# Zero fills of a dilated attention branch moved from GpSimd to VectorE, and its attention steps issued at more places of the dense work

## The chip, the cores and the metric

The kernel runs on one core of one Trainium2 chip. The metric is device time in microseconds (us) of one execution; several runs are taken and their median is used. One further execution was recorded by the hardware profiler, and all rows below are from that one.

## The reference

One layer of a decoder trunk in float32, 512 tokens of width 1024. Cut to what matters here:

```python
h = _rms(x, norm1_g[layer])
(a_q, a_k, a_v, i_q, i_k, i_w, b_q, b_kv, b_g, c_qkv, mix_g) = _split_last(h @ w_in[layer], IN_SIZES)
y_a = _dsa_attention(...) @ w_branch_a[layer]      # top-128 keys by an index score, 8 heads
y_b = _nsa_attention(...) @ w_branch_b[layer]      # compressed + selected + window, 8 heads
y_c = _dilated_attention(...) @ w_branch_c[layer]  # 3 groups (windows 128, 512, 2048; steps 1, 4, 16) x 4 heads
g = jax.nn.sigmoid(mix_g).reshape(bsz, seq, 3, D_MODEL)
x = x + (g[:, :, 0] * y_a + g[:, :, 1] * y_b + g[:, :, 2] * y_c) @ w_out[layer]
h = _rms(x, norm2_g[layer])
gate, up = jnp.split(h @ w_ffn_in[layer], 2, axis=-1)
x = x + (jax.nn.silu(gate) * up) @ w_ffn_out[layer]
```

## The kernel before

**Dense work.** Every dense product is made of three matmuls on a high and a low part of each operand (`mm3`, lines 103 to 108). Weights come by DMA on SyncE's queue (`weights`, line 84): a tile `raw` of two 128-row chunks is cast to `whi` on ScalarE (line 81) and the rest `wlo` is taken on VectorE or, in some projections, on GpSimd (line 82); `whi` and `wlo` have six buffers each. These have a higher priority than all else.

**Order of the dense work.** After the first norm come the narrow projections, the index queries, the inputs of the compression, the keys and queries of branch B, then the queries of branch A in two projections of four 128-token tiles, and then nine "dilated" projections of four tiles each (`spill`, line 736, which calls `proj_tm`, line 252): six `cqk_tm` and three `cv_tm`. Each tile is copied from PSUM on ScalarE (line 745), and the result goes to HBM. Then come the gates and merges of the branches, in the order B (`bi` 1), A (`bi` 0), C (`bi` 2), eight column blocks each. `gate(bi, f)` computes a gate block and its tanh `tz` (line 956; three buffers of tag `tm`), `merge(bi, f, tz)` multiplies it by the branch's output block (lines 970 to 973). A merge stands one gate later than its own gate. After them are the output projection, the second norm and the feed-forward part.

**Steps of the attention.** Beside the dense work stands a list of generators; `tick()` (line 119) advances each of them by one step. One is `attention()`, which walks through units of one 128-query tile and two heads: first branch B (with the compressed scores between), then branch A, then the preparation (`c_prep`) and the units (`c_unit`) of the dilated branch C. A unit is cut in parts that go to successive steps: scores, table and softmax; transposes and their copies `pT`; and at the end of four units the products with the values (`ovb`, `ova`, line 541; `ovc`, lines 888 and 893). Another generator does the index scores and the top-k of branch A (`select`, line 413: 48 passes, one per step). `tick()` stands once after each projection tile, twice in each gate, and in the merges of A and every second merge of B and C. So the attention's steps 1 to 4 stand in the second query projection of A, 5 to 28 in the `cqk_tm` and 29 to 40 in the `cv_tm` projections, 41 to 44 in B's first two gates. B's last value product is of step 44, A's of step 61; `ready` (line 1008) would issue what is missing before a merge.

**What sets the order on an engine.** The Tile framework orders the instructions of each engine when it compiles: it takes what its own timeline expects to be ready, the earlier in the program's text first (high priority ahead of that), and gives out buffers as it expects them free. A step's place in the text is thus a rank and no barrier, neither forward nor back. On the chip each engine then runs its list in order.

**Zero fills.** `c_prep` makes, for each of two halves and two heads, a tile `pt12` of 128 x (2 x 4 x 128) elements (three buffers) and zeroes it on GpSimd (line 825). The units copy transposed probabilities of groups 1 and 2 into it (lines 876 and 878): query tile `i` writes 32(i + 1) rows of its 128 columns, so the last tile writes all 128 rows. Its memory is that of the pool `ab`, which branches A and B use before.

Of the kernel before, what the change touches and what calls it, by code (L numbers as in the profile page):

```python
# [22 lines left out]
NT = S // 128  # L23
# [8 lines left out]
C_CQ, C_CK, C_CV, C_MIX = 2268, 3036, 3804, 4572  # L32
# [35 lines left out]
def block_kernel(ctx: ExitStack, tc: tile.TileContext, x, norm1_g, norm2_g, w_in, qk_norm_g, cmp_pos, cmp_w,  # L68
                 w_ba, w_bb, w_bc, w_out, w_fi, w_fo, rel_bias, onehot, masks, out):
    nc = tc.nc  # L70
# [13 lines left out]
    def weights(w, segs, kcs, per=2, pool=()):  # L84

        res = {}
        width = sum(n for _, n in segs)
        with tc.high_priority():
            for k0 in kcs[::per]:
                raw = wp.tile([128, per, width], F32, name="raw", tag="raw", bufs=5)  # L90
                o = 0
                for c0, n in segs:
                    nc.sync.dma_start(raw[:, :, o:o + n],
                                      w[k0 * 128:(k0 + per) * 128, c0:c0 + n].rearrange("(k p) c -> p k c", p=128))
                    o += n
                hi = wp.tile([128, per, width], F32R, name="whi", tag="whi")
                lo = wp.tile([128, per, width], F32R, name="wlo", tag="wlo")
                split(hi, lo, raw, nc.gpsimd if pool and k0 // per % 4 in pool else None)
                for j in range(per):
                    res[k0 + j] = (hi[:, j, :], lo[:, j, :])  # L100
        return res

    def mm3(ps, pairs, k0=0, n=None):
        n = n or len(pairs)
        for j, ((ah, al), (bh, bl)) in enumerate(pairs, k0):
            nc.tensor.matmul(ps, ah, bh, start=(j == 0), stop=False)  # L106
            nc.tensor.matmul(ps, ah, bl, start=False, stop=False)  # L107
            nc.tensor.matmul(ps, al, bh, start=False, stop=(j == n - 1))  # L108
# [7 lines left out]
    def start(gen):  # L116
        tasks.append(gen)

    def tick():
        for g in list(tasks):  # L120
            try:
                next(g)
            except StopIteration:
                tasks.remove(g)
# [79 lines left out]
    def mm_tile():  # L204
        return mmp.tile([128, S], F32, name="pm", tag="mm")
# [43 lines left out]
        return bass.AP(tensor=tab.tensor, offset=tab.offset + hi - 1, ap=[list(tab.ap[0]), [-1, hi - lo]])  # L249


    def proj_tm(segs, evac, then=None):
        width = sum(n for _, n in segs)
        wk = weights(w_in, segs, list(range(KC)), pool=PP)
        for t in range(NT):
            ps = mm_tile()
            ts = slice(t * 128, (t + 1) * 128)
            mm3(ps[:, 0:width], [((xh[:, k, ts], xl[:, k, ts]), wk[k]) for k in range(KC)])
            evac(t, ps)
            tick()  # L260
        if then is not None:
            start(then())

# [20 lines left out]
    def tmt(name):  # L284
        return ap_.tile([128, NT, 256], F32, name=name, tag="tm", bufs=3)

    def norm_heads(tm, c0, nh):

        ss = ty.tile([128, 16], F32, name="ss", tag="ss")
        v4 = tm[:, :, c0:c0 + 64 * nh].rearrange("p t (h d) -> p t h d", d=64)  # L290
        for t in range(0, NT, 2):
            sq = ap_.tile([128, 2, 256], F32, name="sq", tag="sq", bufs=1)
            nc.scalar.activation(sq[:, :, 0:64 * nh], tm[:, t:t + 2, c0:c0 + 64 * nh], AF.Square)
            nc.vector.tensor_reduce(out=ss[:, t * nh:(t + 2) * nh].rearrange("p (t h) -> p t h", h=nh),
                                    in_=sq[:, :, 0:64 * nh].rearrange("p t (h d) -> p t h d", d=64), op=ALU.add,
                                    axis=AX.X)
        r = rstd(ss, NT * nh, 1.0 / 64)
        r4 = r[:, 0:NT * nh].rearrange("p (t h) -> p t h", h=nh).unsqueeze(3).to_broadcast([128, NT, nh, 64])
        nc.vector.tensor_tensor(out=v4, in0=v4, in1=r4, op=ALU.mult)
# [432 lines left out]
    dC = dp.tile([6, 128, NT, 256], F32, name="dC")  # L732
    dV = dp.tile([3, S, 256], F32, name="dV")
    cmap = {}

    def spill(name, segs, dst, nh):
        t_ = tmt(name)

        def then():
            if nh:  # L740
                norm_heads(t_, 0, nh)
            nc.sync.dma_start(dst, t_)
            yield

        proj_tm(segs, lambda t, ps: nc.scalar.copy(t_[:, t, :], ps[:, 0:256]), then=then)

    c_in = {}
    c_jobs = [(hf, g, s) for hf in range(2) for g in range(3) for s in "qk"]
# [37 lines left out]
    def c_prep(hf, cz, ld):  # L786
        for g in range(3):
            for s in "qk":
                if hf == 1:
                    c_load()  # L790
                    yield
                t_ = c_in.pop((hf, g, s))
                ps = tr_cols(t_, 0)
                if g == 0:
                    ld[s, g] = (near_queries if s == "q" else near_keys)(hf, cz, ps)
                    if len(c_jobs) > 6:
                        c_load()
                    yield
                    continue
                cq = cz.tile([128, S], F32, name="cq", tag="cq", bufs=8)  # L800
                dst = cq
                if s == "q":
                    dst, ps = cq.rearrange("p (i r w) -> p i r w", i=NT, r=4), ps.rearrange("p (i w r) -> p i r w", i=NT, r=4)
                elif g:
                    dst, ps = cq.rearrange("p (r u) -> p r u", r=4), ps.rearrange("p (u r) -> p r u", r=4)
                nc.scalar.activation(dst, ps, AF.Copy, scale=(gain8[:, 4:5] if s == "q" else gain[:, 5:6]))
                ld[s, g] = cq
                if len(c_jobs) > 6:
                    c_load()
                yield  # L810
            rows = dV[g, :, 128 * hf:128 * hf + 128]
            v_ = cz.tile([128, NT, 128], F32, name="c_v", tag="cv", bufs=6)
            nc.sync.dma_start(v_, rows.rearrange("(u r) c -> u r c", r=NT) if g else
                              rows.rearrange("(t p) c -> p t c", p=128))
            ld["v", g] = v_
        for j in range(2):
            h = 2 * hf + j
            tab = cz.tile([128, S], F32, name="ctab", tag="ctab", bufs=4)
            for r in range(4):
                rows = tab[32 * r:32 * r + 32]  # L820
                vec_table(rows[:, 0:256], 16 + h, V_C0 + r, [[4, 32], [1, 256]])
                vec_table(rows[:, 256:384], 20 + h, V_C1, [[1, 32], [1, 128]])
                vec_table(rows[:, 384:512], 24 + h, V_C2, [[1, 32], [1, 128]])
            pt = cz.tile([128, 2, NT, 128], F32, name="pt12", tag="pt12", bufs=3)
            nc.gpsimd.memset(pt, 0.0)
            ld["tab", j], ld["pt", j] = tab, pt

    def c_unit(hf, i, j, ld, d):
# [130 lines left out]
    def merge(bi, f, tz):  # L959
        nk = KC // 2 if bi < 2 else 2  # L960
        os_ = outs[bi]
        cs = slice(128 * (f % 2), 128 * (f % 2) + 128)
        th, zi = tz[:, 0, :], tz[:, 1, :]
        if f % 2 == 0:
            wys["w"] = weights(wbs[bi], [(f // 2 * 256, 256)], list(range(nk)))
        if bi != 1:
            nc.sync.dma_start(zi, dz[f])
        wy = wys["w"]
        py = mm_tile()
        mm3(py, [((wy[k][0][:, cs], wy[k][1][:, cs]), (os_[k][:, 0, :], os_[k][:, 1, :])) for k in range(nk)])  # L970
        if bi == 0 or f % 2:
            tick()
        nc.vector.scalar_tensor_tensor(out=th, in0=th, scalar=1.0, in1=py, op0=ALU.add, op1=ALU.mult)
        if bi != 1:
            eng = nc.vector if bi == 2 and f > KC - 3 else nc.gpsimd
            eng.tensor_tensor(out=th, in0=th, in1=zi, op=ALU.add)
        if bi != 2:
            nc.sync.dma_start(dz[f], th)
        else:
            nc.scalar.mul(zs["h"][:, f, :], th, 0.5)  # L980
            nc.vector.scalar_tensor_tensor(out=zs["l"][:, f, :], in0=th, scalar=0.5, in1=zs["h"][:, f, :].bitcast(F32),
                                           op0=ALU.mult, op1=ALU.subtract)
# [15 lines left out]
    cn = 0  # L998
    for hf in range(2):
        for g in range(3):  # L1000
            spill("cqk_tm", [(C_CQ + 256 * g + 128 * hf, 128), (C_CK + 256 * g + 128 * hf, 128)], dC[cn], 4)
            cmap["q", hf, g], cmap["k", hf, g] = (cn, 0), (cn, 128)
            cn += 1
    for g in range(3):
        spill("cv_tm", [(C_CV + 256 * g, 256)], dV[g].rearrange("(t p) c -> p t c", p=128), 0)
    zx = ExitStack()

    def ready(bi):
# [19 lines left out]
    for m_ in due:  # L1028
        merge(*m_)
# [78 lines left out]
    for c in range(0, DFF, 256):  # L1108
# [7 lines left out]
        for j in range(2):  # L1116
# [7 lines left out]
            f = c // 128 + j  # L1124
# [40 lines left out]
```

## Time and profile before

| | |
|---|---|
| median of 3 runs | 996.48 us (994.18 to 1000.4) |
| the profiled execution: its time | 995.54 us |
| the profiled execution: first to last instruction | 993.8 us |
| mean granted TensorE clock | 0.993 of full speed |
| TensorE busy | 974.3 us, 98% |
| VectorE, ScalarE, GpSimd busy | 568.1, 437.5, 175.4 us |

1.74 us of the profiled execution lie outside the span. In the rows, PE is TensorE, PEld its weight load, DVE VectorE, ACT ScalarE, POOL GpSimd, SPq the DMA queue of SyncE; L12 is line 12 of the kernel. In a table by stretch each engine has its busy time and, in brackets, its instructions; PEclk is the clock granted, 1.00 for 2.4 GHz and 0.50 for 1.2 GHz.

### The profile page before, as it was taken

To read this page: it belongs to the slowest core of one execution; us is meant where nothing else is said; L and a number is where in the kernel's file an instruction comes from. 1 tells how busy PE (TensorE), PEld (TensorE's weight loads), DVE (VectorE), ACT (ScalarE), POOL (GpSimd) and SP (SyncE) were. 2 spreads that over 40 slices of the span, in tenths; PEclk is the share of its full clock that TensorE was granted. 3 is DMA by queue.
4 is the path that set the end of the run, shared out by engine and by line. 5 is a ranking of instruction groups with operands and counts; after the bars stand their busy time and mean duration, and the time that the engine had idled before them with its cause. 6 is when DMAs were issued, how large, how long until landed. Compare 5 with 4: busy or idle time off the path is not lost.

```text
span 993.8 us, 16076 instructions
## 1 busy us (share of the span) xinstructions
PE 974.3 (98%) x5887; PEld 827.0 (83%) x5887; DVE 568.1 (57%) x1277; ACT 437.5 (44%) x956; POOL 175.4 (18%) x156
## 2 busy tenths in 40 slices
PE   6999999999999999989999999999999999999998
PEld 6889999899887578858777899988888888888886
DVE  6699999766665655665764654544344444422321
ACT  5544555755665555554543434433233233322220
POOL 4135555543100202231110312000000000000000
PEclk9999999999999899989999999999999999999999
DMA  8541344433232334346613462233333323332421
GB/s 210 122 128 44 85 119 132 123 109 122 90 104 67 85 117 138 107 141 193 180 62 97 140 210 86 85 94 108 96 85 105 107 85 91 110 97 96 138 75 42
DMA packets 119264, 109.91 MB, mean 111 GB/s; under 512 B 19931, under 2 KB 105234, under 8 KB 119186
## 3 DMA queue, kind: packets, MB, share of 16 engines
q1 hardware_dynamic: 116994, 107.85, 37.4%
q10 hardware_dynamic: 2192, 1.05, 0.4%
q8 instruction: 46, 0.75, 0.3%
q14 instruction: 32, 0.26, 0.1%
HBM read 96.66 MB, written 12.21 MB: 110 GB/s over the span
## 4 chain that ended last, share of the span: by engine, by line
PE 96%; DMA 1%; DVE 1%; ACT 1%; issue 0%; SPq 0%; DVEq 0%; ACTq 0%
PE pf L108 14%; PE pf L107 14%; PE pf L106 14%; PE pm L107 13%; PE pm L106 13%; PE pm L108 13%; PE tr L111 5%; PE ovb L541 2%; PE lg L363 2%; PE lg L364 2%; PE ova L541 1%; PE lg L843 1%; DMA raw<-in_w_in 1%; PE ovc L888 1%; PE lg L838 0%
## 5 line engine op out<-in xcount | busy, mean ns | idle before, releaser
L82 DVE TENSOR_TENSOR wlo<-raw,whi 128x512 fp32r<-128x512 f32 (+1 forms) x243 | 182.5, 756 | 147.7 <-ACT whi L81 146.6
L81 ACT CAST whi<-raw 128x512 fp32r<-128x512 f32 (+1 forms) x288 | 176.8, 619 | 173.9 <-PE pf L108 78.6
L107 PE MATMUL pm<-wlo,xh 128*128 128x256 f32 (+1 forms) x512 | 145.9, 288 | 0.3 <-DVE wlo L82 0.3
L108 PE MATMUL pm<-whi,xl 128*128 128x256 f32 (+1 forms) x512 | 145.3, 286 | 0.5 <-POOL xl L82 0.5
L106 PE MATMUL pm<-whi,xh 128*128 128x256 f32 (+1 forms) x512 | 145.7, 289 | 0.0
L107 PE MATMUL pf<-xl,whi 128*128 128x512 f32 (+1 forms) x384 | 142.6, 372 | 0.1
L106 PE MATMUL pf<-xh,whi 128*128 128x512 f32 (+1 forms) x384 | 142.5, 372 | 0.0
L108 PE MATMUL pf<-xh,wlo 128*128 128x512 f32 (+1 forms) x384 | 142.0, 371 | 0.0
L107 PEld LDWEIGHTS pm<-wlo,xh 128*128 128x128 f32 x512 | 98.5, 193 | 1.9 <-issue 0.8
L108 PEld LDWEIGHTS pm<-whi,xl 128*128 128x128 f32 x512 | 98.7, 193 | 1.4 <-POOL xl L82 0.8
L106 PEld LDWEIGHTS pm<-whi,xh 128*128 128x128 f32 x512 | 98.3, 194 | 0.4
L107 PE MATMUL pm<-xl,whi 128*128 128x512 f32 x224 | 88.8, 396 | 0.0
L108 PE MATMUL pm<-xh,wlo 128*128 128x512 f32 x224 | 88.6, 395 | 0.0
L106 PE MATMUL pm<-xh,whi 128*128 128x512 f32 x224 | 88.4, 395 | 0.0
L107 PEld LDWEIGHTS pf<-xl,whi 128*128 128x128 f32 x384 | 72.3, 188 | 12.8 <-DVE xl L82 0.3
L108 PEld LDWEIGHTS pf<-xh,wlo 128*128 128x128 f32 x384 | 72.2, 188 | 12.6
L106 PEld LDWEIGHTS pf<-xh,whi 128*128 128x128 f32 x384 | 72.2, 188 | 12.3
L82 POOL TENSOR_TENSOR wlo<-raw,whi 128x512 fp32r<-128x512 f32 x45 | 62.2, 1402 | 111.6 <-ACT whi L81 100.8
L106 PE MATMUL pf<-whi,hh 128*128 128x512 f32 x176 | 69.4, 395 | 0.0
L108 PE MATMUL pf<-whi,hl 128*128 128x512 f32 x176 | 69.4, 395 | 0.0
L107 PE MATMUL pf<-wlo,hh 128*128 128x512 f32 x176 | 69.4, 395 | 0.0
L562 ACT ACTIVATE p<-p,m 128x128 f32<-128x128 f32 (+3 forms) x96 | 53.9, 562 | 28.6 <-DVE m L547 26.4
(312 smaller groups left out, 1702.3 us busy)
## 6 DMA issues: line engine op xcount, KB each, us to landing
raw<-in_w_in SPq DMA_DIRECT2D x92, 256.0 KB, 3.0
raw<-in_w_ffn_in SPq DMA_DIRECT2D x88, 256.0 KB, 2.9
raw<-in_w_ffn_out SPq DMA_DIRECT2D x44, 256.0 KB, 2.8
raw<-in_w_in SPq DMA_DIRECT2D x52, 128.0 KB, 2.4
x<-in_x SPq DMA_DIRECT2D x8, 512.0 KB, 5.9
tab<-dvec SPq DMA_DIRECT2D x16, 256.0 KB, 3.3
dz<-tz SPq DMA_DIRECT2D x16, 256.0 KB, 2.4
tz<-dz SPq DMA_DIRECT2D x16, 256.0 KB, 3.3
```

Of the source, the lines that this page charges most:

```text
L81: nc.scalar.copy(dst_hi, src)
L82: (eng or nc.vector).tensor_tensor(out=dst_lo, in0=src, in1=dst_hi.bitcast(F32), op=ALU.subtract)
L106: nc.tensor.matmul(ps, ah, bh, start=(j == 0), stop=False)
L107: nc.tensor.matmul(ps, ah, bl, start=False, stop=False)
L108: nc.tensor.matmul(ps, al, bh, start=False, stop=(j == n - 1))
L111: nc.tensor.transpose(dst, src, ident[0:src.shape[0], 0:src.shape[0]])
L363: nc.tensor.matmul(lg, qs, k[:, 0, 0:w], start=True, stop=False)
L364: nc.tensor.matmul(lg, qs, k[:, 1, 0:w], start=False, stop=stop)
L541: mm = nc.tensor.matmul(ov[64 * j:64 * j + 64, 128 * b:S], v(b), pts[j][:, 4 * b:3 * b + NT, :], start=first and b == 0, stop=last and b = ...
L562: nc.scalar.activation(p[:, 0:w], p[:, 0:w], AF.Exp, bias=m[:, 0:1], scale=-1.0, accum_out=m[:, 1:2])
L843: nc.tensor.matmul(lg[32 * r:32 * r + 32, c:c + n], ld["q", g][hp, 128 * i + 32 * r:128 * i + 32 * r + 32], ld["k", g][hp, 128 * r:128 * r ...
L888: nc.tensor.matmul(ov[h, 128 * b_:128 * q1], ld["v", 0][:, b_, h], d["pt", jj][:, 2 * b_:b_ + q1, :], start=b_ == 0, stop=False)
```

## The change

1. The zero fill goes to VectorE and covers the first three of the four query tiles (128 x 768 elements for 128 x 1024), since the last tile's columns are written whole.
2. Each of the nine dilated projections has five steps for four: two after its first tile (`more=1`).
3. Every merge has a step: four more in B's merges (the even blocks), and four in C's, where all steps are done by then.

```diff
-    def proj_tm(segs, evac, then=None):
+    def proj_tm(segs, evac, then=None, more=0):
...
-            tick()
+            for _ in range(1 + (t < more)):
+                tick()
...
-    def spill(name, segs, dst, nh):
+    def spill(name, segs, dst, nh, more=0):
...
-        proj_tm(segs, lambda t, ps: nc.scalar.copy(t_[:, t, :], ps[:, 0:256]), then=then)
+        proj_tm(segs, lambda t, ps: nc.scalar.copy(t_[:, t, :], ps[:, 0:256]), then=then, more=more)
...
-            nc.gpsimd.memset(pt, 0.0)
+            nc.vector.memset(pt[:, :, 0:NT - 1, :], 0.0)
...
-        if bi == 0 or f % 2:
-            tick()
+        tick()
...
-            spill("cqk_tm", [...], dC[cn], 4)
+            spill("cqk_tm", [...], dC[cn], 4, 1)
...
-        spill("cv_tm", [(C_CV + 256 * g, 256)], dV[g].rearrange("(t p) c -> p t c", p=128), 0)
+        spill("cv_tm", [(C_CV + 256 * g, 256)], dV[g].rearrange("(t p) c -> p t c", p=128), 0, 1)
```

After it the attention's steps 5 to 34 stand in the `cqk_tm`, 35 to 49 in the `cv_tm` projections, and B's first gate begins with step 50.

## Rows read from the trace of the kernel before

**Rows 1.** The page: the engines' shares, and the chain that ended last, by engine.
```profile
PE 974.3 (98%) x5887; PEld 827.0 (83%) x5887; DVE 568.1 (57%) x1277; ACT 437.5 (44%) x956; POOL 175.4 (18%) x156
PE 96%; DMA 1%; DVE 1%; ACT 1%; issue 0%; SPq 0%; DVEq 0%; ACTq 0%
```

**Rows 2.** The table by stretch over the span up to 990 us: length, busy time of PE, PEld, DVE, ACT and POOL, PEclk, DMA share, GB/s.
```profile
0.00:15.00 15.00, 6.16 (x25) 5.25 (x26) 8.77 (x24) 8.56 (x18) 6.67 (x16) 1.00 0.87 243
15.00:322.00 307.00, 307.00 (x2292) 280.36 (x2292) 237.21 (x603) 172.41 (x421) 107.59 (x79) 1.00 0.39 105
322.00:340.00 18.00, 15.73 (x83) 9.07 (x82) 9.43 (x35) 10.42 (x29) 0.67 (x1) 0.81 0.23 68
340.00:430.00 90.00, 90.00 (x463) 71.68 (x462) 56.66 (x150) 51.17 (x124) 21.52 (x21) 1.00 0.41 120
430.00:446.00 16.00, 11.45 (x54) 6.89 (x53) 10.39 (x19) 7.44 (x17) 4.50 (x6) 0.79 0.53 150
446.00:990.00 544.00, 543.89 (x2979) 453.76 (x2979) 244.94 (x451) 187.54 (x352) 34.45 (x35) 1.00 0.36 109
```

**Rows 3.** The same table inside the two holes.
```profile
326.00:331.20 5.20, 3.57 (x23) 2.49 (x22) 3.57 (x10) 4.20 (x11) 0.59 (x1) 1.00 0.34 104
331.20:338.00 6.80, 6.26 (x24) 3.37 (x26) 1.66 (x6) 1.90 (x5) 0.08 (x1) 0.50 0.13 38
431.90:433.60 1.70, 0.14 (x1) 0.00 (x0) 1.70 (x1) 0.36 (x3) 1.70 (x3) 1.00 0.45 124
433.60:440.20 6.60, 3.93 (x17) 3.13 (x18) 4.60 (x11) 3.25 (x8) 1.58 (x2) 0.50 0.25 75
```

**Rows 4.** The timeline of the second hole (start, duration, engine, line, tile, shapes, and in brackets the idle time of the engine before it and what ended that).
```profile
431.34 1.16 POOL L557 TENSOR_TENSOR tabm<-tab,topm 128x512 f32<-128x512 f32 x1 [0.70 <-DVE m L563]
431.37 4.02 DVE L564 TENSOR_SCALAR p<-p,m 128x384 f32<-128x384 f32 x1
432.44 2.74 POOL L825 MEMSET pt<- 128x1024 f32 x3
435.31 0.67 DVE L547 CUSTOM_DVE_ANT_0 p<-lg,tabm 128x512 f32<-128x512 f32 x1
435.54 0.87 PE L111 MATMUL tr<-ident,p 128*128 128x128 f32 x3 [3.49 <-DVE p L564]
436.59 0.41 DVE L564 TENSOR_SCALAR p<-p,m 128x384 f32<-128x384 f32 x1
```

**Rows 5.** The timeline of VectorE and GpSimd 2 us earlier, where the same operation stands beside one GpSimd operation.
```profile
428.99 1.64 POOL L557 TENSOR_TENSOR tabm<-tab,topm 128x512 f32<-128x512 f32 x1 [0.24 <-DVE m L563]
429.53 1.26 DVE L564 TENSOR_SCALAR p<-p,m 128x256 f32<-128x256 f32 x1
```

**Rows 6.** Groups by line and shape: prices of a fill and of VectorE operations of one result.
```profile
L825 POOL MEMSET pt<- 128x1024 f32 x4 | 3.7, 962 | 10.8 <-PE ovc L893 10.8
L140 DVE MEMSET mhalf<- 128x16 f32 x1 | 0.1, 72 | 0.8 <-PEq L1156 0.8
L547 DVE CUSTOM_DVE_ANT_0 p<-lg,tab 128x128 f32<-128x128 f32 x24 | 6.8, 288 | 16.9 <-PE lg L364 15.0 <-PE tr L111 1.2 <-DMA tab<-dvec 0.7
L547 DVE CUSTOM_DVE_ANT_0 p<-lg,tab 128x512 f32<-128x512 f32 x16 | 10.7, 688 | 9.4 <-PE lg L364 7.0 <-PE tr L111 2.1
```

**Rows 7.** Timelines of single engines, in order of time: the last pass of the top-k; the copies of the 22nd `cqk_tm` tile and of the third and fourth `cv_tm` tile; the first value product of B's third pair; the activation of B's second gate; B's last value product; the activation of B's fourth gate.
```profile
163.33 0.68 DVE L418 MATCH_REPLACE8 work<-m,work 128x512 f32<-128x512 f32 x1
216.29 0.37 ACT L745 COPY cqk_tm<-pm 128x256 f32<-128x256 f32 x1 [0.20 <-PE pm L108]
236.72 0.37 ACT L745 COPY cv_tm<-pm 128x256 f32<-128x256 f32 x1 [0.84 <-PE pm L108]
242.18 0.37 ACT L745 COPY cv_tm<-pm 128x256 f32<-128x256 f32 x1
285.09 2.38 PE L541 MATMUL ovb<-pT,bv 128*64 128x512 f32 x16
298.92 0.60 ACT L956 ACTIVATE tz<-pm 128x512 f32<-128x512 f32 x1
333.18 4.53 PE L541 MATMUL ovb<-pT,bv 128*64 128x512 f32 x16 [0.35 <-ACT pT L530]
344.99 0.60 ACT L956 ACTIVATE tz<-pm 128x512 f32<-128x512 f32 x1 [0.25 <-DMA dz<-tz]
```

**Rows 8.** TensorE's timeline in the middle of the sum of one gate (`pm`), with transposes and scores of B between.
```profile
292.12 0.40 PE L108 MATMUL pm<-xh,wlo 128*128 128x512 f32 x1
292.36 0.71 PE L111 MATMUL tr<-ident,p 128*128 128x128 f32 x5
293.08 0.45 PE L106 MATMUL pm<-xh,whi 128*128 128x512 f32 x1
```

**Rows 9.** The timelines of GpSimd and VectorE at the fourth fill.
```profile
511.18 0.96 POOL L825 MEMSET pt<- 128x1024 f32 x1 [10.76 <-PE ovc L893]
512.48 1.08 DVE L82 TENSOR_TENSOR oT<-ovc,oT 128x512 fp32r<-128x512 f32 x1 [1.23 <-ACT oT L81]
```

**Rows 10.** TensorE's timeline in a gate with nothing between: four dense matmuls follow from 312.76 to 313.44 us, of which the first and the last.
```profile
312.76 0.39 PE L106 MATMUL pm<-xh,whi 128*128 128x512 f32 x1
...
313.44 0.39 PE L106 MATMUL pm<-xh,whi 128*128 128x512 f32 x1
```

More of the change, by code (lines that the diff above doesn't have):

```diff
@@ L1000, in block_kernel @@
         for g in range(3):
-            spill("cqk_tm", [(C_CQ + 256 * g + 128 * hf, 128), (C_CK + 256 * g + 128 * hf, 128)], dC[cn], 4)
+            spill("cqk_tm", [(C_CQ + 256 * g + 128 * hf, 128), (C_CK + 256 * g + 128 * hf, 128)], dC[cn], 4, 1)
             cmap["q", hf, g], cmap["k", hf, g] = (cn, 0), (cn, 128)
```

## The prediction

> **What bounds the kernel now.** I read the shares first: TensorE is busy for 974.3 of 993.8 us, and 96% of the chain that ended last is TensorE [rows 1]. No other engine can set the time, so the question is only where TensorE stands still or runs slowly. The table by stretch answers it: before 15 us it lacks 8.84 us while the first loads come, in the 544 us from 446 on 0.11 us, and nothing in two stretches of 307 and 90 us. What is left, besides the last 4 us of the span, are two holes, 322 to 340 us (2.27 us idle) and 430 to 446 us (4.55 us idle) [rows 2]. Inside each the granted clock falls from 2.4 to 1.2 GHz after TensorE has been partly idle: in the first it was busy for 3.57 of 5.2 us before the fall, in the second for 0.14 of 1.7 us. While low it worked for 6.26 and 3.93 us [rows 3]; at full clock this is half the time, so the low clock cost about 3.1 and 2.0 us. The holes thus cost 2.27 + 3.1 = 5.4 us and 4.55 + 2.0 = 6.5 us, 11.9 us together. That is all that a change of order can give: 995.54 - 11.9 = 983.6 us, 1.2% faster.
>
> The first hole is the wait for branch B's last value product (333.18 us), the second that for branch A's. By then the dense work has run ahead as far as its buffers go: B's second gate is activated at 298.92 us, and the fourth, two gates ahead of its place, only at 344.99 us, when a `tz` buffer came back [rows 7]. The holes close if the attention comes earlier against the dense work.
>
> **The zero fill: what it removes.** In the second hole VectorE's scaling of a 128x384 block takes 4.02 us, where the other head's block of the same unit takes 0.41 us. It begins beside a GpSimd `tabm` and ends 0.2 us after the third of three fills, which GpSimd runs from 432.44 to 435.18 us; TensorE's next transpose waits for it [rows 4]. Two us earlier the same operation stood beside one `tabm` alone and took 1.26 us, ending 0.16 us after that [rows 5]. So VectorE cannot finish this operation while GpSimd works, and the fills alone hold it for the 2.74 us that they take. I take off 2.7 us, as the whole chain behind it (table, exponential, transposes, value product) hangs on it and TensorE has nothing else. The bounds are 0 and 4.02 - 0.41 = 3.6 us.
>
> The Trainium skill ("SBUF — State Buffer", section "Who interferes with whom") names the cause, a port pair that VectorE's two-port operations and GpSimd share, and says that the pair is held for a whole instruction by whoever issues first. By that rule the scaling, waiting since 431.37 us, would have the pair when `tabm` ends at 432.50 us, before the fills, and moving these would give nothing here. The row speaks against it, as VectorE was held through three further instructions. The same section has it that on trn2 a VectorE instruction with at most one SBUF input outside the two-port modes does not contend with GpSimd; no run here shows it for a fill.
>
> **The zero fill: what it adds.** No row has a VectorE fill of this size. From below: 128x16 takes 72 ns. VectorE's one-result operation goes from 288 ns at 128 columns to 688 ns at 512, so 1.04 ns a column [rows 6]; 768 columns make 0.80 us, and with the 55 ns that 72 - 16 x 1.04 leaves, 0.86 us. From above, GpSimd's 962 ns for 1024 columns [rows 6] would do. Three fills cost VectorE 2.6 us, and they fall where the first ones fall now, since `pt12` lies in the memory of branches A and B and is free only near A's end. There VectorE is the path: it is busy for 4.60 of the 6.6 us up to 440.2 [rows 3], and its free 2 us lie mostly behind A's last scaling. A fill queued ahead of that delays all behind it: the rest of A's softmax, and with it TensorE's last transposes and A's value product. Bounds: 0 if all three come behind A's last scaling, 2.6 us if all stand ahead. The fills rank behind A's own steps, so only those that fit a gap which the compiler expects stand ahead; there is about one such gap, so I take one fill, 0.9 us. The fourth waits for branch C's first value products; just behind them VectorE stops for 1.23 us [rows 9], which covers 0.86 us. If it is queued earlier it blocks VectorE; that is a rival below. GpSimd loses 3.7 us [rows 6], of which nobody waits for more than the scaling above.
>
> Net for the fill: -2.7 + 0.9 = -1.8 us. The clock cost of the hole I leave: it keeps 4.55 - 1.8 = 2.7 us of idle time, and the first hole shows the clock falling after 5.2 - 3.57 = 1.6 us of it [rows 3]. The bounds on that are 0 and 2.0 us of gain.
>
> **The steps.** The change issues 13 steps before they are issued now: nine in the dilated projections, four in B's merges. A step brings scores, softmax, transposes, value products, and on SyncE's queue its table, query and `c_in` loads. None is added, so the work is equal; what could change is the order. I say that it hardly does, since in the order that the trace shows a step's place holds nothing back, and its work trails that place. The two rows: the last of the 48 top-k passes belongs to attention step 31, whose place is after the third `cv_tm` tile (copied at 236.72 us), and it ran at 163.33 us, 73 us early. The value product of step 32, whose place is after the fourth `cv_tm` tile (242.18 us), ran at 285.09 us, 43 us late; that of step 44, placed after B's second gate (298.92 us), at 333.18 us, 34 us late [rows 7]. An attention that is late with its place already stands first in rank against the dense matmuls beside it, and indeed its transposes cut into the middle of a gate's sum [rows 8]: they stand where their operands were expected. With the change step 32's place is after the 22nd `cqk_tm` tile (216.29 us), 26 us further forward, of a step that is late by 43 us. What paces it is its own chain of score, softmax, transpose and copy through two or three buffers each, and the change leaves that alone. The loads on SyncE's queue are moved past weight loads in rank only: they wait for buffers which the same late steps give back, so I cost them at 0; the price if that is wrong is in the second rival. The four steps in C's merges find an empty list.
>
> So I take 0 for this part. Bounds: below, both holes closed (-11.9 us with the fill's share in it); above, a new order that makes the first hole, 5.4 us, half as long again, +2.7 us.
>
> **Sum:** 995.54 - 1.8 + 0 = 993.7 us for a profiled execution. That lies 0.9 us below the median of the runs, 996.48 us, which themselves lie 6 us apart; less than 1% is not told from no change here. The likeliest case's own range is 989 (first hole as it is, fills free, clock held: -2.7 - 2.0 = 990.8, and some of the first hole) to 999 us (all fills in the path, +2.7, and the spread of the runs).
>
> **Rivals.**
> 1. The earlier places do pull the attention forward: B ends before the dense work runs dry, and A too. For it: early in the attention (before 150 us) it is not yet late, and a lead won there could be kept; the passes of the top-k show VectorE taking work far ahead. Against it: the 43 us. Both holes go, the clock stays at 2.4 GHz: 983.6 us. If only the first goes, 993.7 - 5.4 = 988.3 us.
> 2. VectorE's queue blocks. A fill waits in it for its buffer, and the weights' low parts queue behind. GpSimd's fourth fill had its queue waiting 10.76 us for branch C's value products [rows 9]. TensorE takes three dense matmuls in 0.68 us [rows 10], so a weight tile of two chunks in 1.36 us; a gate pair holds four of the six `wlo` tiles, two are spare, so from about 2.7 us of wait on it starves. At 10.76 us: 8.1 us idle, and a low clock at the first hole's 3.1 us: 993.7 + 11.2 = 1004.9 us. A load moved forward on SyncE's queue that waits for its buffer would act alike. Against it: GpSimd had nothing else to do there, so its wait shows when it was queued and not when VectorE would queue it; an order made by readiness puts it about where it can run.
> 3. The change does nothing at all: the scaling is held by something else in GpSimd's queue, and the fills find cover: 995.5 us. This is inside the likeliest case's range and can't be told from it by time.
>
> **How the numbers follow.** Likeliest case with rival 3: 0.72. Rival 1: 0.20, of which 0.12 with both holes gone and 0.08 with one. Rival 2: 0.08. The predicted time is 993.7 us. For 8 in 10 the range takes the likeliest case and most of rival 1: 984 to 999 us; it leaves out rival 2 and the lower edge of both holes closed. Faster by over 1% (below 985.6 us) needs both holes nearly closed: the 0.12 of rival 1, and 0.04 of the likeliest case for a gain in the new order that these rows don't show. Slower by over 1% (above 1005.5 us) needs rival 2 at its full price and a little more: 0.05. Within 1%: 0.79.
>
> **What would show it.** No VectorE scaling above 1.3 us near A's end; four VectorE fills of about 0.86 us, three of them close to A's last value product. If the steps do nothing, B's last value product still comes at about 333 us, 34 us after B's second gate, and the hole before it is still there with its fall to 1.2 GHz. If the hole is gone and the value product comes ahead of the third gate, rival 1 is right and I have misread what the places do. If a VectorE wait of some us with low parts queued behind stands before a TensorE gap, it is rival 2. The prediction is wrong in size if the clock holds in the second hole.

## The result, and the profile after

The changed kernel takes 1005.72 us (median of 5 runs, 1005.21 to 1006.71) beside 994.68 us of the kernel before on the same chip; the ratio is 1.0099, 95% interval 1.0079 to 1.0118. So it is 1% slower, 9.8 us by this ratio (the two medians are 11.0 us apart), and lies above the range that was given. The profiled execution took 1005.21 us with a span of 1003.4 us. Beside the kernel before, lines of the code from 261 on stand one lower.

The shares of the engines and the chain, to be read against [rows 1]:

```profile
PE 974.9 (97%) x5887; PEld 829.4 (83%) x5887; DVE 562.4 (56%) x1281; ACT 437.9 (44%) x956; POOL 172.9 (17%) x152
PE 85%; DVE 7%; DMA 3%; SPq 1%; issue 1%; ACT 1%; POOL 1%; DVEq 0%; POOLq 0%; ACTq 0%
```

TensorE does the same work in nearly the same busy time (974.3 us before), so of the 9.6 us by which the span grew 9.0 are time in which it stands still. The chain, 96% TensorE before, now runs for 15% over others. The table by stretch, columns as in [rows 2], shows where:

```profile
15.00:322.00 307.00, 305.08 (x2279) 277.66 (x2279) 233.13 (x601) 171.33 (x418) 108.84 (x79) 1.00 0.38 105
322.00:340.00 18.00, 15.57 (x100) 10.17 (x99) 11.57 (x42) 12.64 (x35) 1.91 (x3) 1.00 0.28 74
430.00:446.00 16.00, 11.99 (x53) 7.22 (x53) 11.67 (x23) 9.04 (x19) 2.95 (x3) 0.84 0.59 169
446.00:458.80 12.80, 12.80 (x77) 10.53 (x76) 2.86 (x4) 3.05 (x5) 2.36 (x2) 0.94 0.53 138
458.80:464.40 5.60, 1.89 (x40) 1.24 (x38) 4.38 (x19) 2.76 (x7) 0.00 (x0) 1.00 0.40 105
464.40:482.00 17.60, 13.80 (x102) 10.43 (x103) 10.37 (x35) 9.55 (x21) 0.10 (x1) 0.52 0.59 181
482.00:990.00 508.00, 507.95 (x2717) 427.90 (x2716) 219.88 (x383) 170.68 (x317) 29.02 (x31) 1.00 0.34 103
```

The two known holes are hardly changed: 2.43 us idle for 2.27, 4.01 for 4.55. New is a **third hole**, 458.8 to 482 us: 3.71 + 3.80 = 7.5 us idle, and 13.8 us of work at a granted clock of 0.52, nearly all at 1.2 GHz, which at full clock would have taken some 6.6 us less (an estimate, 0.48 of 13.8 us). Before, these stretches had no idle time and the full clock. (The sum of busy time shows little of the 6.6 us: the first hole ran at full clock this time, which gives 3.1 us back, and for the rest no row was found.) A small loss is in the first 322 us, 1.92 us idle for none.

In the hole TensorE executes only branch C's first units and their preparation; the last dense matmul before it starts at 458.81 us, the next at 479.32 us. What the dense work waits for stands in the timelines of TensorE, GpSimd (the addition of a merge, L976) and ScalarE (the activation of a gate, L957):

```profile
458.81 0.39 PE L108 MATMUL pm<-oT,wlo 128*128 128x512 f32 x1
479.32 0.78 PE L106 MATMUL pm<-xh,whi 128*128 128x512 f32 x1
444.02 3.04 POOL L976 TENSOR_TENSOR tz<-tz 128x512 f32<-128x512 f32 x2 [13.05 <-DVE tz L973]
449.35 1.29 POOL L976 TENSOR_TENSOR tz<-tz 128x512 f32<-128x512 f32 x1 [2.29 <-DVE tz L973]
481.90 1.30 POOL L976 TENSOR_TENSOR tz<-tz 128x512 f32<-128x512 f32 x1 [31.26 <-DMA tz<-dz]
477.69 0.60 ACT L957 ACTIVATE tz<-pm 128x512 f32<-128x512 f32 x1 [0.21 <-DMA dz<-tz]
```

Three merges of branch A are added up by 450.6 us. A `tz` buffer is free when its result has been stored to `dz`; the next gate's activation comes at 477.69 us, when the first of these stores has landed. Until then no dense matmul could start: the dense sums (`pm`) have three PSUM buffers (line 196), and two gates' sums, whose last matmuls start at 426.50 and 454.76 us, and the merge's of 458.81 us hold all three until the activations at 477.69 and 478.44 us and the merge's product at 478.40 us. ScalarE itself stands idle for only 0.21 us there: its list has branch C's operations ahead of the activation, so the compiler, it seems, expected the buffer late as well. SyncE's queue tells why it is late, after and, in the second fence, before:

```profile
446.82 5.10 SPq L246 DMA_DIRECT2D ctab<-dvec  x11
452.02 0.53 SPq L756 DMA_DIRECT2D c_in<-dC  x1
452.59 1.87 SPq L814 DMA_DIRECT2D c_v<-dV  x3
454.50 5.86 SPq L246 DMA_DIRECT2D ctab<-dvec  x9
...
467.56 4.33 SPq L246 DMA_DIRECT2D ctab<-dvec  x9
473.64 0.52 SPq L756 DMA_DIRECT2D c_in<-dC  x1
474.26 1.57 SPq L978 DMA_DIRECT2D dz<-tz  x3
475.96 0.53 SPq L756 DMA_DIRECT2D c_in<-dC  x1
477.63 1.92 SPq L968 DMA_DIRECT2D tz<-dz  x3
```

```profile
447.29 0.34 SPq L978 DMA_DIRECT2D dz<-tz  x1
447.90 1.23 SPq L246 DMA_DIRECT2D ctab<-dvec  x3
449.92 0.39 SPq L93 DMA_DIRECT2D raw<-in_w_in  x1
450.35 7.09 SPq L246 DMA_DIRECT2D ctab<-dvec  x15
457.54 0.53 SPq L755 DMA_DIRECT2D c_in<-dC  x1
458.17 0.56 SPq L978 DMA_DIRECT2D dz<-tz  x1
```

Before, the first store was issued at 447.29 us, right behind its addition, and the next two at 458.17 and 459.92 us, with 6, 24 and 24 of branch C's 48 table loads (`ctab`, mostly 0.42 us an issue) ahead of them. After, all 48 stand ahead of the three stores, with values and inputs of branch C, and these are issued from 474.26 us on, 24 us after the last of the three additions ended. The queue runs in its order, and this order changed.

### The profile page after: what moved, and what is told of

The parts are those of the page before. It is cut to its first block, busy times and chain, and to the rows that moved or that the text cites. A ratio compares the mean times of both kernels' runs of the same rounds, so it can differ in the third digit from the quotient of the medians.

```text
span 1003.4 us, 16078 instructions
## 1 busy us (share of the span) xinstructions
PE 974.9 (97%) x5887; PEld 829.4 (83%) x5887; DVE 562.4 (56%) x1281; ACT 437.9 (44%) x956; POOL 172.9 (17%) x152
## 4 chain that ended last, share of the span: by engine, by line
PE 85%; DVE 7%; DMA 3%; SPq 1%; issue 1%; ACT 1%; POOL 1%; DVEq 0%; POOLq 0%; ACTq 0%
PE pf L107 14%; PE pf L108 14%; PE pf L106 13%; PE pm L107 11%; PE pm L106 10%; PE pm L108 10%; PE tr L111 4%; PE ovb L542 2%; PE lg L364 2%; PE lg L365 2%; DVE work L419 1%; DVE m L418 1%; DMA raw<-in_w_in 1%; DMA c_v<-dV 1%; SPq L246 1%
## 5 line engine op out<-in xcount | busy, mean ns | idle before, releaser
L82 DVE TENSOR_TENSOR wlo<-raw,whi 128x512 fp32r<-128x512 f32 (+1 forms) x243 | 175.7, 729 | 152.3 <-ACT whi L81 142.6
```

Source lines behind the costliest of these rows:

```text
L82: (eng or nc.vector).tensor_tensor(out=dst_lo, in0=src, in1=dst_hi.bitcast(F32), op=ALU.subtract)
```

## The experiments

The theory on which they rest: the additional steps move branch C's preparation ahead in rank, its loads therefore ahead of the merges' `dz` and `tz` transfers in SyncE's queue, and the dense work runs out of `tz` buffers. Rivals are named in the expectations. Differences between two rows carry both intervals, some 2 to 4 us together. The ratio of each kernel to the kernel before, with TensorE's idle time and granted clock in 424 to 484 us of its profiled execution (4.55 us and 0.94 before):

| | ratio, 95% interval | idle, us | clock |
|---|---|---|---|
| changed kernel | 1.0099 [1.0079, 1.0118] | 11.59 | 0.80 |
| e1 fill alone | 1.0055 [1.0034, 1.0076] | 4.19 | 0.94 |
| e2 steps alone | 1.0127 [1.0093, 1.0161] | 11.33 | 0.78 |
| e3 fill, steps in merges | 1.0029 [1.0010, 1.0049] | 4.12 | 0.94 |
| e12 fill, steps in projections | 1.0097 [1.0065, 1.0130] | 11.05 | 0.80 |
| e4 changed, C held 13 steps | 1.0052 [1.0036, 1.0069] | 6.75 | 0.91 |
| e5 changed, 12 table issues | 1.0057 [1.0036, 1.0079] | 9.46 | 0.91 |
| e6 changed, tables on ScalarE's queue | 1.0076 [1.0046, 1.0106] | 9.05 | 0.80 |
| e9 changed, dz/tz first | 1.0029 [1.0011, 1.0047] | 6.20 | 0.91 |
| e10 changed, dz/tz on GpSimd's queue | 1.0053 [1.0033, 1.0073] | 5.95 | 0.89 |
| e11 fill alone, dz/tz first | 1.0006 [0.9983, 1.0028] | 4.19 | 0.94 |
| e7 fill alone, 12 table issues | 1.0007 [0.9991, 1.0023] | 6.15 | 0.94 |
| e8 before, 12 table issues | 1.0026 [1.0008, 1.0044] | 6.36 | 0.94 |
| e13 fill on ScalarE | 1.0005 [0.9990, 1.0019] | 5.45 | 0.94 |
| e14 fill on GpSimd, three tiles | 1.0003 [0.9986, 1.0021] | 4.91 | 0.97 |
| e15 fill on ScalarE, dz/tz first | 0.9959 [0.9941, 0.9978] | 4.30 | 0.97 |
| e16 as e15, with the steps | 0.9989 [0.9973, 1.0005] | 3.49 | 0.97 |
| e17 before, dz/tz first | 1.0029 [1.0013, 1.0045] | 5.51 | 0.94 |
| e18 as e15, 12 table issues | 1.0030 [1.0015, 1.0046] | 7.16 | 0.94 |

### Which part makes the hole (e1, e2, e3, e12)

The fill alone is the one line of the diff in `c_prep`; e2 is the rest of the diff; e3 has the fill and the tick in every merge, e12 the fill and `more=1`.

> The kernel before with the first part of the change alone: zero fill on VectorE for three query tiles of four. Theory Q (the steps moved branch C's preparation ahead of weight and dz loads in SyncE's queue, and that queue made the new hole at 446 to 480 us): no third hole, A's last scaling no longer held for 4 us, 991 to 993 us, 2 to 3.5 us below the kernel before. Rival F (the fills on VectorE made the new hole, by holding weight low parts behind them): the hole at 446 to 480 us is there, 1003 to 1006 us.

> The changed kernel with the zero fill back on GpSimd, so the steps alone. Theory Q: the third hole is there as in the changed kernel, and the fills hold A's last scaling again: 1005.7 + 2.7, 1007 to 1009 us. Rival F: no third hole, 993 to 996 us.

> Fill on VectorE and the additional steps in the merges alone (four count before branch C), none in the dilated projections. Theory Q: what counts is by how many steps C's preparation is moved ahead, 4 here against 13, so a small part of the hole at most: 992 to 997 us. Rival M (it is the steps in the merges, which stand beside the dz transfers, that make the hole, and those in the projections are harmless, as the attention trails them): 1003 to 1006 us.

> The fill on VectorE and the nine additional steps in the dilated projections, none in the merges. Theory: the nine of the thirteen suffice to bring C's loads ahead of three merges' dz transfers: the hole of the changed kernel, 1003 to 1006 us. If it is the sum of both groups that counts: between 998 and 1002 us.

The third hole is there with the nine steps in the projections (e2, e12) and not without them (e1, e3): 11 us idle against 4. That part went as expected, and the four steps in B's merges cost nothing that shows (e3 is not slower than e1; its 998.18 us lie above its range, which counted on the fill's gain). On the fills the first expectation missed: the fill alone is 0.55% slower, not 2 to 3.5 us faster, and without making the hole, so neither theory had it. Beside the steps 1.0127 to 1.0099 would be a gain of 2.8 us, the size that was expected, but the two intervals overlap, so that a gain is not shown.

### Is it the place of branch C's preparation (e4)

```diff
         cz = czx.enter_context(tc.tile_pool(name="cz", bufs=1, reuse_waits="tile"))
         lds = [{}, {}]
+        yield from wait(13)
         yield from c_prep(0, cz, lds[0])
```

> The changed kernel with 13 empty steps ahead of branch C's preparation, so that B's and A's steps stand as early as in the changed kernel and C's preparation as late as in the kernel before. Theory Q: no third hole, within 1 us of the kernel with the fill alone, 991 to 993 us. Rival E (the earlier places of B and A are what costs, for instance by moving their loads): the hole stays, 1003 to 1006 us.

1.0052 against 1.0055 of the fill alone: with C's preparation back at its old place 4.7 us of the change's 9.8 are gone, and the time does not show that the earlier places of A and B cost anything. It cannot exclude 2 us of it either, and the profile of e4 has stops that e1 has not, the longest of 3.07 us for a `c_in` load at 467 us. The level of 991 to 993 us was wrong, since it rested on the fill.

### Is it the queue, and what in it (e5, e6, e9, e10, e11)

Fewer issues (e5): one load for the four row groups of a table instead of four. Another queue (e6): `nc.scalar.dma_start` for the tables.

```diff
-            for r in range(4):
-                rows = tab[32 * r:32 * r + 32]
-                vec_table(rows[:, 0:256], 16 + h, V_C0 + r, [[4, 32], [1, 256]])
...
+            vec_table(tab[:, 0:256], 16 + h, V_C0, [[1, 4], [4, 32], [1, 256]])
+            vec_table(tab[:, 256:384], 20 + h, V_C1, [[0, 4], [1, 32], [1, 128]])
+            vec_table(tab[:, 384:512], 24 + h, V_C2, [[0, 4], [1, 32], [1, 128]])
```

> The changed kernel with the tables of branch C loaded by 12 issues on SyncE's queue for 48, same bytes. Theory Q (the queue is held by the number of issues, 0.42 us each): 36 issues less free 15 us of the queue between 430 and 480 us, the dz and weight loads come that much earlier, and of the 21.6 us that idle time and low clock cost in 424 to 484 us some 14 go: 992 to 1000 us. Rival L (it is the bytes, the landing of many short pieces, or the wait for buffers, and not the issues): 1003 to 1006 us, hole as before.

> The changed kernel with the 48 table loads of branch C issued on ScalarE's queue. Theory Q: SyncE's queue is free for dz and weight loads and the third hole shrinks, but ScalarE has to issue 48 loads of some 0.4 us, which may delay its copies: 993 to 1002 us. Rival L: as the changed kernel or slower, 1004 to 1010 us.

e5 goes part of the way, 4.2 us of the 9.8, and misses its range by 1.6 us. e6 lies in rival L's range, and its interval overlaps with that of the changed kernel. SyncE's queue and a gate's activation on ScalarE in e5 and then in e6:

```profile
452.31 4.62 SPq L246 DMA_DIRECT2D ctab<-dvec  x5
457.03 1.63 SPq L976 DMA_DIRECT2D dz<-tz  x3
462.44 1.30 ACT L955 ACTIVATE tz<-pm 128x512 f32<-128x512 f32 x2 [11.97 <-DMA dz<-tz]
```

```profile
448.87 1.80 SPq L978 DMA_DIRECT2D dz<-tz  x2
453.18 0.32 SPq L978 DMA_DIRECT2D dz<-tz  x1
467.19 9.71 SPq L756 DMA_DIRECT2D c_in<-dC  x3
476.95 1.09 SPq L968 DMA_DIRECT2D tz<-dz  x2
476.97 0.59 ACT L957 ACTIVATE tz<-pm 128x512 f32<-128x512 f32 x1
```

In e5 the twelve issues, of 128 rows each, hold the queue for 11.8 us where the 48 hold it for 21.3 us; the stores still stand behind all the tables. Here the wait is seen on the chip: ScalarE stands idle for 11.97 us until a store has landed, and TensorE waits 5.77 us for the activation behind it. In e6 the queue is free of tables and the three stores are out by 453.5 us, and yet the activation comes at 476.97 us and the hole stays. No idle time stands before the activation: ScalarE's list has branch C's operations ahead of it, as in the changed kernel, though the stores were issued early. So a queue that is free on the chip does not close the hole by itself; the order that the compiler gave the other engines holds the dense work too, and why it kept that order in e6 is open. The `tz` loads are late in e6 as well, behind three `c_in` loads, which take 9.71 us where one issue takes 0.53: in the trace the last two wait for TensorE's transposes, which by the code give back their buffer. So the transfers themselves were moved, by rank (e9, e11) and to another queue (e10):

```diff
         if bi != 1:
-            nc.sync.dma_start(zi, dz[f])
+            with tc.high_priority():
+                nc.sync.dma_start(zi, dz[f])
...
         if bi != 2:
-            nc.sync.dma_start(dz[f], th)
+            with tc.high_priority():
+                nc.sync.dma_start(dz[f], th)
```

> The changed kernel with the merges' dz and tz transfers at high priority: the same transfers on the same queue of SyncE, put ahead in rank of branch C's loads. Theory S (the third hole comes from the dz and tz transfers standing behind branch C's loads in SyncE's in-order queue, whether these take issue time or wait for a buffer; the tz buffers come back late, and the dense matmuls with them): the hole at 457 to 482 us, some 14 us with its low clock, goes: 991 to 999 us. Rival P (TensorE's own order holds C's chain ahead of the dense work because C's steps rank earlier, the transfers are late only as a consequence): the hole stays, 1003 to 1006 us.

> The changed kernel with the merges' dz and tz transfers issued on GpSimd's queue instead of SyncE's. Theory S: the hole goes as with the high priority, 991 to 1000 us. Rival P: 1003 to 1006 us.

> The kernel with the fill alone, and the dz and tz transfers at high priority. Theory S: with these transfers ahead, the place of C's preparation no longer matters, so that this and the changed kernel with the same edit agree within 2 us. Rival P: this one stays at 998 to 1001 us while the other is 3 us or more above it.

The queue of e9, and in the second fence its row of the table by stretch between 446 and 482 us, where the changed kernel had 28.5 us of work in 36:

```profile
446.14 0.37 SPq L980 DMA_DIRECT2D dz<-tz  x1
447.63 0.38 SPq L980 DMA_DIRECT2D dz<-tz  x1
448.22 0.33 SPq L969 DMA_DIRECT2D tz<-dz  x1
451.84 0.42 SPq L980 DMA_DIRECT2D dz<-tz  x1
```

```profile
446.00:482.00 36.00, 33.50 (x226) 26.17 (x226) 16.72 (x43) 15.19 (x29) 4.80 (x4) 0.91 0.67 192
```

The same loads, the same steps, the same queue, and the stores are out at 446 to 452 us instead of 474 us: 7.0 us of the 9.8 come back. The same edit on the kernel before brings nothing (e17, 1.0029), so this is not a gain that any kernel would have from it. On GpSimd's queue (e10) 4.6 us come back, with 1001.39 us just above the range. With the transfers first, the kernels with and without the steps stand 2.3 us apart (e9, e11), which the intervals do not tell from nothing, where without it they stand 4.4 us apart. That the third hole comes from the place of these transfers is shown, and rival P, by which the rank of C's steps makes it whatever the transfers do, falls. Not parted is how much of it the queue makes on the chip (e5 shows that wait) and how much the engines' lists, which the compiler builds around the transfers that it expects late (e6). What is left of it in e9 is one stop of 2.50 us for a `c_in` load and 3.4 us of cost at the low clock behind it.

### Where the fill's gain goes (e7, e8, e13, e14)

In the trace of e1 branch A's last block is cast on ScalarE at 439.74 us, 3.3 us earlier than before (443.01 us). Then TensorE stops twice, which it did not before; its timeline, then VectorE's:

```profile
443.68 0.33 PE L838 MATMUL lg<-cks,cqs 128*128 128x128 f32 x1 [1.21 <-DVE cks L781]
444.39 0.50 PE L106 MATMUL pm<-oT,whi 128*128 128x512 f32 x1 [0.39 <-DVE tz L973]
442.12 1.50 DVE L781 SCALAR_TENSOR_TENSOR cks<-tr,gain_qk,cks 64x512 fp32r<-64x512 f32 x2 [0.35 <-ACT cks L779]
443.65 1.29 DVE L973 SCALAR_TENSOR_TENSOR tz<-tz,pm 128x512 f32<-128x512 f32 x2
```

The second half of C's first scores now stands ahead of the third merge in TensorE's list, and `cks` ahead of the merges' `tz` in VectorE's. 1.6 us of idle time and 3.4 us of work at 1.2 GHz behind it (1.7 us) take the 3.3 us back. The changed kernel has the same two stops:

```profile
443.22 0.33 PE L839 MATMUL lg<-cks,cqs 128*128 128x128 f32 x1 [1.21 <-DVE cks L782]
```

The stops take a gain back, but make no loss of 5.5 us: e7 and e11 have both too and are not told from the kernel before (1.0007 and 1.0006). 0.8 us of idle time stands at 544 to 550 us, the profiled execution of e1 is only 2.9 us longer than that of the kernel before, and the rest of that loss is open. Two other fills tell whether the gain goes there: on ScalarE (e13), where they come to stand between `cqs` and `cks`, and a shorter one left on GpSimd (e14).

```diff
-            nc.gpsimd.memset(pt, 0.0)
+            nc.scalar.mul(pt[:, :, 0:NT - 1, :], ident.unsqueeze(1).unsqueeze(1).to_broadcast([128, 2, NT - 1, 128]), 0.0)
```

> The kernel before with the fill (three query tiles) on ScalarE. Open: the fill on VectorE ends branch A 3.3 us earlier, as forecast, and yet gains nothing; its trace shows TensorE waiting 1.21 us for cks and 0.39 us for tz right behind A, with 3.4 us of work at 1.2 GHz after it. Theory T (these two stops give the gain back; they come because VectorE's list now has the low part of cks ahead of the merges' products): on ScalarE the fills stand between cqs and cks, VectorE's list keeps the merges' products first, the stops are gone and the gain stays: 989 to 993 us. Rival U (an A that ends earlier gains nothing wherever the fill is, as the dense work behind it waits for other things): 994 to 998 us.

> The kernel before with the fill left on GpSimd, three query tiles for four: 768 columns for 1024, some 0.72 us for 0.96 us each. Theory: A's last scaling is held as long as the three fills last, so it ends 0.7 us earlier, TensorE's list is as before and the gain stays: 0.5 to 1 us below the kernel before, about 994 us. Rival: nothing moves, 994.5 to 995 us; only the profile (length of that scaling, 3.3 us for 4.0 us) can tell them apart.

```profile
431.58 2.10 POOL L825 MEMSET pt<- 128x768 f32 x3
430.52 3.38 DVE L564 TENSOR_SCALAR p<-p,m 128x384 f32<-128x384 f32 x1
```

These lines of e14 settle the mechanism: three fills of 2.10 us for 2.74, and the scaling takes 3.38 us for 4.02, shorter by the same 0.64 us; without fills on GpSimd it takes 1.35 us. The time cannot tell 0.6 us from nothing, as expected. In e13 `tz` comes ahead of `cks` and the two stops shrink to one of 0.31 us; the kernel is 5 us faster than e1, but not faster than before, in rival U's range: a `c_in` load then stops TensorE for 3.04 us at 467 us, with a low clock behind it. Theory T holds for the stops and fails in size.

> The kernel with the fill alone on VectorE, and 12 issues for 48 of the tables. Reading of its trace so far: A ends 3.3 us earlier as forecast, and the gain goes where TensorE waits 1.21 us for VectorE's cks and 0.39 us for tz at 443 us and runs at 1.2 GHz for 3.4 us behind that. If that is all, the queue has no part in it, 998 to 1001 us. If the queue costs in this order too, 992 to 996 us.

> The kernel before with 12 issues for 48 of the tables. In its trace no TensorE stop hangs on SyncE's queue between 440 and 600 us, so 993 to 996 us. If the number of issues matters in that order too, 985 to 991 us.

e7 came out in its second branch, that the queue costs in this order too: 12 table issues bring the fill alone back by 4.8 us, though the trace of e1 showed no stop at the queue. e8 came out in neither: they cost the kernel before 2.6 us. Small moves in this order shift stops of 1 to 3 us about; these two are not explained.

### Both mended (e15 to e18)

> As the fill on ScalarE, with the dz and tz transfers at high priority as well. Theory T: 988 to 993 us, no worse than the fill on ScalarE alone. Rival U: 994 to 998 us.

> The changed kernel with its additional steps, the fill on ScalarE and the dz and tz transfers at high priority. If the two mechanisms (the transfers behind C's loads, and cks ahead of tz) are the whole loss, it agrees with the same kernel without the additional steps within 2 us: 989 to 995 us. If the steps cost something else, 996 us or more.

> The kernel before, its fills on GpSimd, with the dz and tz transfers at high priority. It parts the gain of the kernel with the fill on ScalarE and these transfers ahead (991.7 us, 3 us below the kernel before). If the fill is worth what the held scaling measured (2.7 us) and the transfers only keep it, this one is at 994 to 996 us. If the transfers alone are the gain: 991 to 992 us.

> The fill on ScalarE, the dz and tz transfers at high priority, and 12 table issues for 48. In the trace without the last, TensorE still stops 0.40 and 1.50 us for c_in loads, which stand behind table issues in SyncE's queue. If these stops go: 989 to 991 us. If the queue's length no longer matters: 991 to 992.5 us.

e15 beats both kernels: 991.65 us, 0.41% below before. Neither edit does it alone, the fill on ScalarE (1.0005) or the transfers first (1.0029, missed by 2 us); with the transfers first, taking the fill off GpSimd is worth 0.7%. The profiled executions of e17 and e15 are 4.1 us apart; of these, 2.67 us are the scaling that is no longer held (4.03 and 1.36 us), and the second hole is at 1.2 GHz for half as long. The steps on top (e16) cost 3.0 us, more than the 2 us within which the two were to agree. Of these 1.15 us show; TensorE's timeline of e16, with stops that every kernel with the steps in the projections has and none without them:

```profile
159.22 0.33 PE L111 MATMUL tr<-ident,pc 128*128 128x128 f32 x1 [0.34 <-DVE pc L634]
169.81 0.30 PE L111 MATMUL tr<-ident,pc 128*128 128x128 f32 x1 [0.81 <-DVE pc L634]
```

e18 was to gain up to 2 us and loses 7. Its queue and TensorE's stop:

```profile
464.65 0.37 SPq L93 DMA_DIRECT2D raw<-in_w_in  x1
469.14 0.34 SPq L966 DMA_DIRECT2D tz<-dz  x1
470.05 0.56 SPq L755 DMA_DIRECT2D c_in<-dC  x1
474.05 0.66 PE L111 MATMUL tr<-ident,c_in 128*128 128x128 f32 x4 [3.28 <-DMA c_in<-dC]
```

Here the transfer put first is the blocker: the queue stands from 465.0 to 469.1 us at a `tz` load, which waits for the landing of a `dz` store issued at 463.03 us, and the `c_in` load behind it comes 3.28 us late for TensorE. That reading was not tested by a further run.

## Why the prediction was wrong, point by point

**The bound was read rightly, and too narrowly.** TensorE's idle time and clock decide, and its work did not change. But the look went to the two holes that were there. The stretch from 446 us on, with 0.11 us of idle time [rows 2], was taken as safe; that it stayed full depended on stores issued between branch C's loads.

**The step that failed** is in the part on the steps: "The loads on SyncE's queue are moved past weight loads in rank only ... so I cost them at 0." They were moved past the `dz` stores and `tz` loads of the merges, which the prediction did not name. Its own argument that rank is no barrier holds for an engine whose late work trails its place; in the queue an earlier rank stood as an earlier issue, mostly of 0.42 us and 48 of them for the tables, all ahead of the stores where 6 were ahead of the first one before. In place of the 0, the runs show 1.0052 with C's place restored, 1.0029 with the transfers ahead and 1.0099 without either, so that 4.7 to 7.0 us of the 9.8 are the price of that term. The second rival had the mechanism in one sentence (a load moved forward on SyncE's queue) and its price, 1004.9 us, is near the result. That is luck: the price was worked out for a wait of VectorE's queue, and the fills there hold up nothing that shows.

**What the steps do to the attention was right.** B's last value product starts at 334.14 us (333.18 before), 34.7 us after B's second gate at 299.42 us; the first hole keeps 2.43 us of idle time. Rival 1 is out. The cost of the two small stops at 159 and 170 us (158 and 168 us in the changed kernel, 1.2 us together) was not foreseen.

**The removal of the fill was right in size, and did not stay.** Predicted: the scaling held for 2.7 us less. Measured, VectorE's timeline of the changed kernel:

```profile
429.83 1.35 DVE L565 TENSOR_SCALAR p<-p,m 128x384 f32<-128x384 f32 x1
434.55 2.31 DVE L826 MEMSET pt<- 128x768 f32 x3
504.83 0.70 DVE L826 MEMSET pt<- 128x768 f32 x1 [1.78 <-PE ovc L894]
```

4.02 - 1.35 = 2.67 us. A fill takes 0.70 to 0.77 us, not 0.86, and none of the three stands ahead of A's last scaling at 433.95 us, where one was taken (0.9 us); the bound 0 was the right end. It is given back within 10 us, in the kernel with the fill alone and in the changed kernel, since the compiler's order behind A changed too: the step "TensorE has nothing else", by which the whole chain moves up, looked only as far as A's end. That GpSimd's fills hold the scaling was read rightly as well, though [rows 5] has a block of 256 columns and not the same operation: the block of 384 takes 1.35 us beside `tabm` alone. By the Trainium skill ("SBUF — State Buffer", section "Who interferes with whom") whoever issues first gets the shared port pair for the whole instruction; by that rule the fills behind `tabm` could not have held the scaling. e14, where 0.64 us less of fills shorten it by 0.64 us, goes with [rows 4] and against that.

**A slip in the sum.** The 0.9 us below the median of 996.48 us belong to the profiled execution before, 995.54 us; the forecast of 993.7 us lies 2.8 us below that median.

## What to carry to other kernels

When a change moves steps in a program that a compiler orders by rank, list for each in-order queue what the moved transfers now stand in front of, and ask who waits for those; a stretch that is full today can be full only because of that order. A stop removed upstream is a gain only when the next operations in every engine's list are also ready then, so follow the chain some microseconds past the hole. The lists of the other engines are built around the time at which the compiler expects a transfer, so that a queue made free does not always free the work behind it (e6). Short transfers that return buffers (here stores of one tile) are worth a priority of their own, but one that waits for its own buffer blocks the queue in turn.

## What the runs showed of the hardware that was not expected

- SyncE's queue is mostly held for 0.42 us by a load of 32 rows and for 0.5 to 2.5 us (median 0.80) by one of 128 rows of the same tables in e5, so 48 table loads hold it for 21.3 us and 12 for 11.8 us.
- A VectorE scaling of 128x384 is held through several GpSimd instructions in a row: 1.35 us with `tabm` alone, 3.38 us with 2.10 us of fills, 4.02 us with 2.74 us.
- With the same 2.3 to 2.4 us of idle time in 322 to 340 us, the granted clock of that stretch was 0.81, 0.91 or 1.00 in the profiles, 0.81 in those of the kernel before and of e18, 1.00 in that of the changed kernel and of e8, the kernel before with 12 table issues. Up to 337 us the kernel before, e8, e14 and e18 give all four engines the same lists, and their clocks there are 0.81, 1.00, 0.91 and 0.81. So the 3.1 us that the prediction put on that hole's low clock are not a property of the kernel, and single profiles differ by as much. Whole runs differ with the clock too: among 35 of the kernel before, measured beside e13, the fastest (991.27 us) had a mean clock of 0.998 and the slowest (1000.79 us) 0.990.
